# A hybrid decoder block on one core: a new order of the opening, an earlier projection chunk, and the first queries' scores in two products

## The chip, the cores and the metric

The kernel runs on one core of one Trainium2 chip. The metric is the device time of one execution in microseconds (us); the time of a kernel is the median of its runs. The core has a matrix engine (TensorE, in the profile PE, its weight loads PEld), a vector engine (VectorE, DVE), a scalar engine for copies and functions (ScalarE, ACT), a general engine (GpSimd, POOL) and SyncE (SP), which here only issues DMAs. Each works through its own queue in order and waits on semaphores for the others.

## What is computed

One decoder layer over 512 tokens of width 1024, all in float32:

```
h = rms_norm(x, norm_mix_g)
q_a,k_a,v_a,o_a,i_a,f_a,q_b,k_b,v_b,g_a,g_b = split(h @ w_in)      # 8208 columns
q_a,k_a = silu(causal_conv(concat(q_a,k_a), conv_w))
y_a = sigmoid(o_a) * head_rms_norm(mlstm_chunkwise(q_a,k_a,v_a,i,f))     # 8 heads, 64 wide keys, 128 wide values
y_b = stick_breaking(head_rms_norm(q_b), head_rms_norm(k_b), v_b)        # 8 heads, 128 wide
y = sigmoid(g_a + b) * y_a + sigmoid(g_b + b) * y_b
x = x + y @ w_out
x = x + square(relu(rms_norm(x, norm_mlp_g) @ w_up)) @ w_down
```

The stick-breaking attention takes, for a query t, beta = sigmoid(q.k / sqrt(128)) for all keys before t, and weights v_s with beta_ts times the product of (1 - beta_tj) over the keys j between s and t.

## The kernel before

**Products in three parts.** Every float32 operand is split into an upper part (`hi`, a copy by ACT into a type that TensorE takes) and a lower part (`lo`, value minus `hi`, by DVE). `mm3` (line 119) then issues three matrix products into one accumulator: hi x hi, hi x lo, lo x hi. Nearly all products are 128 x 128 stationary by 512 moving columns.

**Chunks.** A projection of 512 columns is a chunk (`chunk`, line 124): four accumulators of 128 x 512 in the pool `ps_proj` (4 PSUM banks), eight steps k over the 1024 inputs, so 8 x 4 x 3 = 96 products. Weights come in four loads of 256 rows (`stage`, line 103): SP issues the DMA into a `raw` buffer, ACT makes `hi` and DVE makes `lo`. `raw` has two buffers (three from chunk `qkb1` on, line 663), `hi` and `lo` four each.

**The order of the work.** The list `ORDER` (line 60) names steps, and `step` (line 660) issues each: `qka` are the mLSTM's q and k projections with their convolution, `r` its decay tables, `m` its heads, `n` its norm; `qkb`, `T` and `s` are the attention's q and k projections, the transposes of a pair of heads and a head; `va`, `vb`, `oa`, `ga`, `gb` the other projections. The order of the list is a priority: a scheduler places instructions on the engines' queues at compile time, higher priority first, but lets a later step's instructions go ahead where they are ready and an earlier step's aren't. `tc.high_priority` moves instructions up, `tc.issue_after(i)` puts them behind `i` on its engine. A tile whose pool has no free buffer waits for one.

**The opening** (lines 185 to 384) computes `h` transposed (`hT`, upper and lower) and at the same time the first chunk, `va0`. SP loads, for four tiles of 128 tokens, `x` (512 KB each) and, for each 256 rows of `va0`'s weights, `raw_va` (512 KB each), in turns. The string given to `opening` (line 370) is the order on ACT and DVE, written by hand: `q` t squares and sums tile t on ACT and takes root and reciprocal (line 256); `s` t g scales half g of tile t on DVE into `xn`, and PE turns it with four transposes of 128 x 128 (line 263); `u` t g and `l` t g write the upper and lower part of that half of `hT` (ACT, DVE); `w` i and `v` i the upper and lower part of weight pair i; `g` the gate weights. `in_turn` (line 248) puts each step behind the last one on its engine.

PE meanwhile runs filler products on a tile of zeros into the bank `pw` (`keep_warm`, line 229): eight at the start, two after the gain rows, then 1, 5 and 3 after the transposes of (0, 0), (0, 1) and (1, 0) (line 274). `va0`'s accumulators: two of `ps_proj`'s four banks are `gps`, the gain rows, which are read until tile 3 is scaled; accumulators 0 and 1 have the two others. `behind` (line 372) puts the steps k = 4 to 7 of `va0` behind the transposes of tiles 2 and 3.

**An attention head** (`sb_head`, line 548) takes scores of four blocks of 128 queries against their 512, 384, 256 and 128 keys. `SEG` names the segments: j = 0 has 512 columns at offset 0, j = 1 has 384 at 512, j = 3 has 128 at 896, j = 2 has 256 at 1024. Three banks hold them (`half_square`, line 85), so the first 128 queries (j = 3) lie behind j = 1 in the second bank, and half of the third bank is empty. ACT reads each segment twice for sigmoid(z) and sigmoid(-z), POOL masks the diagonal, DVE scans, PE transposes (`zt`) and multiplies with v (`po`).

Of the kernel before, what the change touches and what calls it, by code (L numbers as in the profile page):

```python
# [8 lines left out]
F32 = mybir.dt.float32  # L9
F32R = mybir.dt.float32r  # L10
# [46 lines left out]
C_QB, C_KB, C_VB, C_GA, C_GB = 3088, 4112, 5136, 6160, 7184  # L57


ORDER = ("qka0 r0 r1 qkb0 m0 r2 m1 r3 T0 qkb1 m2 m3 n0 vb0 s0 T1 s1 oa0 s2 s3 qka1 ga0 r4 r5 va1 m4 r6 m5 r7 qkb2 m6 m7 "  # L60
         "n4 T2 qkb3 vb1 s4 s5 T3 gb0 s6 s7 x0 oa1 ga1 gb1").split()


# [1 line left out]
def block_kernel(ctx: ExitStack, tc: tile.TileContext, x, norm_mix_g, w_in, b_if, b_gate, conv_w, mlstm_norm_g,  # L65
# [32 lines left out]
        return at.tile([P, S], F32, tag=tag, name=name, bufs=bufs)  # L98


    last, load_pool, staged = {}, [(wp, "raw", 2)], []

    def stage(k2, srcs, name, ahead=None, pool_raw=None):

        with tc.high_priority(offset=AHEAD if ahead is None else ahead):
            p, tag, bufs = load_pool[len(staged) % len(load_pool)] if pool_raw is None else (pool_raw, "raw", 2)
            staged.append(name)
            raw = p.tile([P, 2, 512], F32, tag=tag, name=f"raw_{name}{k2}", bufs=bufs)
            for c, ap in srcs:
                n = ap.shape[-1]  # L110
                last["load"] = nc.sync.dma_start(out=raw[:, :, c:c + n],
                                                 in_=ap.rearrange("(kk p) n -> p kk n", p=P)).ins
            hi = wp.tile([P, 2, 512], F32R, tag="whi", name=f"whi_{name}{k2}")
            lo = wp.tile([P, 2, 512], F32R, tag="wlo", name=f"wlo_{name}{k2}")
            act.copy(hi, raw)  # L115
            dve.tensor_sub(lo, raw, hi.bitcast(F32))  # L116
        return hi, lo

    def mm3(o, ah, al, bh, bl, start, stop, **kw):
        pe.matmul(o, ah, bh, start=start, stop=False, **kw)  # L120
        pe.matmul(o, ah, bl, start=False, stop=False, **kw)  # L121
        return pe.matmul(o, al, bh, start=False, stop=stop, **kw).ins  # L122

    def chunk(name, src, transposed, lhs=None, staged=None, evac=None, gen=False,
              order=range(4), behind={}):


        acc = {}

        def one(o, k, wh, wl):  # L130
            kk, sl = k % 2, slice(o * P, (o + 1) * P)
            st, sp = k == 0, k == NK - 1
            if transposed:
                mm3(acc[o], wh[:, kk, sl], wl[:, kk, sl], hT[0][:, k, :], hT[1][:, k, :], st, sp)
            else:
                ah, al = (hT[0][:, k, sl], hT[1][:, k, sl]) if lhs is None else lhs(k, sl)
                mm3(acc[o], ah, al, wh[:, kk, :], wl[:, kk, :], st, sp)

        def new(o):
            acc[o] = ps_proj.tile([P, S], F32, tag="pp", name=f"pp_{name}{o}")  # L140

        if evac is not None:
            w = staged or [stage(k2, src(k2), name) for k2 in range(4)]
            def each():
                for o in order:
                    new(o)
                    for k in range(NK):
                        with ExitStack() as es:
                            if k in behind:
                                es.enter_context(tc.issue_after(behind[k]))  # L150
                            one(o, k, *w[k // 2])
                    evac(o, acc[o])
                    yield
            if gen:
                return each()
            list(each())
        else:
            for o in range(4):
# [32 lines left out]
    gx = xp.tile([1, D], F32, name="gx")  # L191
    nc.sync.dma_start(out=gx, in_=norm_mix_g[0:1, :])
    xs, raw_va, va0_src = {}, {}, in_cols((C_VA, 512))
    for i in range(NT):
        xs[i] = xp.tile([P, D], F32, name=f"x_{i}")
        nc.sync.dma_start(out=xs[i], in_=x[0, i * P:(i + 1) * P, :])
        raw_va[i] = (xp if i < 2 else wp).tile([P, 2, 512], F32, tag="raw", name=f"raw_va0{i}", bufs=2)
        last["load"] = nc.sync.dma_start(out=raw_va[i], in_=va0_src(i)[0][1].rearrange("(kk p) n -> p kk n", p=P)).ins
    eps = cst.tile([P, 1], F32, name="eps")
    pool.memset(eps, EPS)  # L200
    one1 = xp.tile([P, P], F32R, name="one1")
# [27 lines left out]
    def keep_warm(n):  # L229
        for i in range(n):  # L230
            pe.matmul(pw, warm[:, :P], warm, start=True, stop=True)
# [31 lines left out]
    def o_scale(t, g):  # L263
        if g == 0:
            xn_[t] = xp.tile([P, D], F32, tag="nx", name=f"xn{t}", bufs=3)
        c = slice(g * S, (g + 1) * S)
        yield dve.scalar_tensor_tensor(xn_[t][:, c], xs[t][:, c], r_[t], gps[g], ALU.mult, ALU.mult).ins
        pt_[t, g] = bank(f"pt{t}{g}")
        for i in range(4):
            k = 4 * g + i  # L270
            turned = pe.transpose(pt_[t, g][:, i * P:(i + 1) * P], xn_[t][:, k * P:(k + 1) * P], ident).ins
        last["turned", t, g] = turned
        with tc.issue_after(turned):
            keep_warm({(0, 0): 1, (0, 1): 5, (1, 0): 3}.get((t, g), 0))

    def h_part(t, g):
        return [h[:, 4 * g:4 * g + 4, t * P:(t + 1) * P] for h in hT], pt_[t, g][:, :].rearrange(
# [7 lines left out]
        (hi, lo), p3 = h_part(t, g)  # L285
        yield dve.tensor_sub(lo, p3, hi.bitcast(F32)).ins

    def o_weights(i):
        va0_w[i] = tuple(wp.tile([P, 2, 512], F32R, tag=f"w{w}", name=f"w{w}_va0{i}") for w in ("hi", "lo"))
        yield act.copy(va0_w[i][0], raw_va[i]).ins  # L290

    def o_weights_lower(i):
        yield dve.tensor_sub(va0_w[i][1], raw_va[i], va0_w[i][0].bitcast(F32)).ins  # L293
# [72 lines left out]
    with tc.issue_after(last["load"]):  # L366
        nc.sync.dma_start(out=wr, in_=w_in[0, :, C_I:C_I + 16].rearrange("(k p) n -> p k n", p=P))
    wg = r4.tile([P, 2, S], F32R, tag="r4", name="wg")[:, :, :].rearrange("p w (k n) -> p (w k) n", k=4)
    pool.memset(wg.bitcast(F32), 0.0)
    opening("q0 s00 s01 u00 l00 w0 v0 q1 s10 u01 l01 s11 u10 l10 w1 v1 u11 l11 q2 s20 s21 w2 v2 u20 l20 q3 s30 u21 "  # L370
            "s31 l21 w3 v3 u30 g l30 u31 l31")
    va0 = chunk("va0", None, False, staged=va0_w, evac=v_evac(v0, "va0"), gen=True,
                behind={k: last["turned", k // 2, 1] for k in range(4, NK)})
    next(va0)
    next(va0)
    next(va0)
# [171 lines left out]
    def sb_head(h, q, k, rq, v):  # L548

        z = half_square(f"zb{h}_")  # L550
        for j, o, n in SEG:
            il = slice((3 - j) * P, (4 - j) * P)
            mm3(part(z, o, n), q[:, 0, il], q[:, 1, il], k[:, 0, :n], k[:, 1, :n], j != 3, True,
                skip_group_check=True)
        b, r = f5(f"b{h}"), f5(f"r{h}")
        for j, o, n in SEG:
            for w, d in ((1, r), (0, b)):
                act.activation(d[:, o:o + n], part(z, o, n), AF.Sigmoid, scale=rq[:, w, 3 - j, h % 2:h % 2 + 1])  # L558
        for j, o, n in SEG:
            d = slice(o + n - P, o + n)  # L560
            pool.affine_select(out=b[:, d], in_=b[:, d], pattern=[[-1, P]], compare_op=ALU.is_gt, fill=0.0, base=0,  # L561
# [87 lines left out]
        pool.memset(oh[:, h, h:h + 1], 1.0)  # L649
    oh_r = at.tile([P, 8, 8], F32R, name="oh_r")  # L650
    pool.tensor_copy(oh_r, oh)
    msk = at.tile([P, S], F32, name="msk")
    pool.memset(msk, 0.0)
    pool.memset(msk[:, 384:], 1.0)
# [336 lines left out]
```

## Time and profile before

| | us |
|---|---|
| median of 3 runs | 816.85 (816.73 to 817.37) |
| the profiled execution | 816.42 |
| span of its instructions | 814.4 |

The profile is of one execution. Its span runs from the first to the last instruction; what is left of the execution's time lies around it. A row of a timeline has the start, the time until the end, engine, line of the kernel, operation, what it writes and reads, the count of instructions merged into the row, and in brackets how long the engine was idle before it and what ended that. Ends of matrix products are modelled and overlap the next one's start, so the distance from start to start tells their cost. In a row of waits stand the engine and line that waited, what it waited for, us in total, times, and the longest. A row of a window has the stretch and its length, then for each engine its busy time and count, PE's clock, the DMA share and GB/s. What a load took from issue to landing is the last number of its row in the DMA view.

### The profile page before, as it was taken

How to read it: one execution, taken by the hardware profiler on the slowest of the kernel's cores; microseconds unless marked ns; L12 is line 12 of the kernel's file. 1: busy time of each engine (PE TensorE's matmuls, PEld its weight loads, DVE VectorE, ACT ScalarE, POOL GpSimd, SP SyncE). 2: the span in 40 equal slices, each digit the busy share in tenths (PEclk: the TensorE clock that was granted, in tenths of full speed). 3: DMA queues.
4: the chain of work that ended last, by engine and by line, in shares of the span. 5: the costliest groups of instructions: out<-in, count | busy, mean ns of one | idle time of the engine just before them, and what ended most of it. 6: DMA issues, size and time to landing. Idle time of an engine off the chain costs nothing.

```text
span 814.4 us, 11569 instructions
## 1 busy us (share of the span) xinstructions
PE 805.7 (99%) x4392; PEld 693.5 (85%) x4392; DVE 599.8 (74%) x828; ACT 457.1 (56%) x681; POOL 164.6 (20%) x216
## 2 busy tenths in 40 slices
PE   8999999999999999999999999999999999999998
PEld 6878887888888887888888888999999899999876
DVE  6669967684598486756753659898689868978995
ACT  6429756654557467545542537576455635755642
POOL 3014323111221240010120101223302330232220
PEclk9999999999999999999999999999999999999999
DMA  9454542343433423522257506987977995999964
GB/s 225 98 155 147 123 77 63 88 98 85 150 93 93 120 62 70 137 72 77 78 182 263 124 1 158 208 177 159 204 228 161 179 208 182 182 198 184 233 120 119
DMA packets 64552, 113.65 MB, mean 140 GB/s; under 512 B 5809, under 2 KB 18401, under 8 KB 64498
## 3 DMA queue, kind: packets, MB, share of 16 engines
q1 hardware_dynamic: 44914, 71.43, 31.6%
q0 software_dynamic: 19584, 41.50, 26.8%
q8 instruction: 34, 0.56, 0.3%
q14 instruction: 20, 0.16, 0.1%
HBM read 110.74 MB, written 2.17 MB: 139 GB/s over the span
## 4 chain that ended last, share of the span: by engine, by line
PE 92%; DVE 5%; ACT 1%; issue 1%; DMA 0%; SPq 0%; DVEq 0%; ACTq 0%
PE pp_qkb L122 4%; PE pp_qkb L120 4%; PE pp_qkb L121 4%; PE pp_yup L120 3%; PE pp_yup L121 3%; PE pp_yup L122 3%; PE ydn L121 2%; PE ydn L122 2%; PE ydn L120 2%; PE pp_qka L120 2%; PE pp_va L121 2%; PE pp_qka L121 2%; PE pp_ga L121 2%; PE pp_vb L122 2%; PE pp_vb L120 2%; PE pp_oa L122 2%
## 5 line engine op out<-in xcount | busy, mean ns | idle before, releaser
L561 POOL TENSOR_SCALAR_AFFINE_SELECT b<-b 128x128 f32<-128x128 f32 x32 | 19.0, 608 | 161.2 <-ACT b L558 161.2
L121 PE MATMUL pp_qkb<-wlo_qkb,hT 128*128 128x512 f32 x128 | 50.2, 392 | 0.0
L122 PE MATMUL pp_qkb<-whi_qkb,hT 128*128 128x512 f32 x128 | 50.1, 394 | 0.0
L120 PE MATMUL pp_qkb<-whi_qkb,hT 128*128 128x512 f32 x128 | 49.4, 392 | 0.0
L767 POOL DMA_DIRECT2D raw_Xup<-in_w_up_dram x24 | 28.9, 1239 | 84.8 <-DVE wlo_p5up L728 37.2
L767 POOL DMA_DIRECT2D raw_Xdn<-in_w_down_dram x18 | 21.6, 1214 | 102.8 <-DVE wlo_p5dn L728 36.4
L566 DVE TENSOR_TENSOR_SCAN r<-r,msk 128x512 f32<-128x512 f32 (+3 forms) x32 | 25.1, 833 | 14.5 <-ACT r L558 14.5
L116 DVE TENSOR_TENSOR wlo_qkb<-raw_qkb,whi_qkb 128x1024 fp32r<-128x1024 f32 x16 | 21.7, 1364 | 13.8 <-ACT whi_qkb L115 13.8
L122 PEld LDWEIGHTS pp_qkb<-whi_qkb,hT 128*128 128x128 f32 x128 | 24.1, 188 | 5.1
L120 PEld LDWEIGHTS pp_qkb<-whi_qkb,hT 128*128 128x128 f32 x128 | 24.1, 188 | 5.1
L121 PEld LDWEIGHTS pp_qkb<-wlo_qkb,hT 128*128 128x128 f32 x128 | 24.1, 188 | 4.7
L913 ACT ACTIVATE uq<-uq 128x512 f32<-128x512 f32 x32 | 20.0, 630 | 12.2 <-DVE uq L912 12.0
L121 PE MATMUL pp_va<-wlo_va,hT 128*128 128x512 f32 x64 | 24.9, 392 | 0.8 <-DVE wlo_va L293 0.8
L120 PE MATMUL pp_ga<-hT,whi_ga 128*128 128x512 f32 x64 | 25.3, 395 | 0.0
L120 PE MATMUL pp_qka<-hT,whi_qka 128*128 128x512 f32 x64 | 25.2, 397 | 0.0
L121 PE MATMUL pp_qka<-hT,whi_qka 128*128 128x512 f32 x64 | 25.2, 394 | 0.0
L121 PE MATMUL pp_wo<-wlo_wo,y 128*128 128x512 f32 x64 | 25.1, 392 | 0.0
L121 PE MATMUL pp_ga<-hT,whi_ga 128*128 128x512 f32 x64 | 25.1, 392 | 0.0
L121 PE MATMUL pp_oa<-hT,whi_oa 128*128 128x512 f32 x64 | 25.1, 392 | 0.0
L122 PE MATMUL pp_oa<-hT,wlo_oa 128*128 128x512 f32 x64 | 25.1, 392 | 0.0
L120 PE MATMUL pp_vb<-whi_vb,hT 128*128 128x512 f32 x64 | 25.1, 392 | 0.0
L121 PE MATMUL pp_gb<-hT,whi_gb 128*128 128x512 f32 x64 | 25.1, 392 | 0.0
(578 smaller groups left out, 2962.1 us busy)
## 6 DMA issues: line engine op xcount, KB each, us to landing
raw_Xup<-in_w_up_dram POOLq DMA_DIRECT2D x24, 512.0 KB, 7.3
raw_Xdn<-in_w_down_dram POOLq DMA_DIRECT2D x18, 512.0 KB, 6.6
raw_qkb<-in_w_in_dram SPq DMA_DIRECT2D x32, 256.0 KB, 3.9
rb<-rows POOLq DMA_DIRECT2D x8, 640.0 KB, 5.5
raw_va<-in_w_in_dram SPq DMA_DIRECT2D x8, 512.0 KB, 5.2
raw_qka<-in_w_in_dram SPq DMA_DIRECT2D x16, 256.0 KB, 6.3
raw_vb<-in_w_in_dram SPq DMA_DIRECT2D x8, 512.0 KB, 4.4
raw_oa<-in_w_in_dram SPq DMA_DIRECT2D x8, 512.0 KB, 4.2
```

The lines of the kernel that those rows point to most:

```text
L116: dve.tensor_sub(lo, raw, hi.bitcast(F32))
L120: pe.matmul(o, ah, bh, start=start, stop=False, **kw)
L121: pe.matmul(o, ah, bl, start=False, stop=False, **kw)
L122: return pe.matmul(o, al, bh, start=False, stop=stop, **kw).ins
L561: pool.affine_select(out=b[:, d], in_=b[:, d], pattern=[[-1, P]], compare_op=ALU.is_gt, fill=0.0, base=0, channel_multiplier=1)
L566: dve.tensor_tensor_scan(kr, kr, msk[:, S - n:][:, ::-1], 1.0, ALU.mult, ALU.max)
L767: pool.dma_start(out=buf[b, j], in_=src(more, j), accum_op=ALU.add)
L913: act.activation(h(r, c), h(r, c), AF.Square)
```

## The change

Four edits.

1. **Opening.** Loads go x0 x1 w0 w1 x2 w2 x3 w3 instead of x0 w0 x1 w1 and so on. The hand-written order takes x1's square and the transposes of tile 1 ahead of the first weights, and splits weight pairs 0 to 2 into halves (`w00` is the first 128 rows of pair 0). Fillers after (0, 1) are three, not five. In `va0` lo x hi stands before hi x lo (`rows_first`, with the roles as in `mm3`'s arguments). Accumulator 2 takes the fillers' bank `pw`, and tile 1's step k = 3 is put behind the transposes of tile 2's first half.
2. **ORDER.** `qka1` moves from behind `s3` to ahead of `s1`.
3. **A third raw buffer** for the third load of `qkb0`, in the pool `at` (`at_once`).
4. **First queries' scores.** In `sb_head` segment j = 3 goes into the empty half of the third bank: q hi against both parts of the keys in one product of 256 columns, then q lo against k hi, 128 columns. ACT copies the first 128 columns to `b`, DVE adds the second 128, and the two sigmoids read `b`.

```diff
-ORDER = ("qka0 r0 r1 qkb0 m0 r2 m1 r3 T0 qkb1 m2 m3 n0 vb0 s0 T1 s1 oa0 s2 s3 qka1 ga0 r4 r5 va1 m4 r6 m5 r7 qkb2 m6 m7 "
+ORDER = ("qka0 r0 r1 qkb0 m0 r2 m1 r3 T0 qkb1 m2 m3 n0 vb0 s0 T1 qka1 s1 oa0 s2 s3 ga0 r4 r5 va1 m4 r6 m5 r7 qkb2 m6 m7 "
...
+            p, tag, bufs = at_once.get((name, k2), (p, tag, bufs))
...
+    at_once["qkb0", 2] = (at, "raw", 1)
...
-    def mm3(o, ah, al, bh, bl, start, stop, **kw):
+    def mm3(o, ah, al, bh, bl, start, stop, rows_first=False, **kw):
         pe.matmul(o, ah, bh, start=start, stop=False, **kw)
-        pe.matmul(o, ah, bl, start=False, stop=False, **kw)
-        return pe.matmul(o, al, bh, start=False, stop=stop, **kw).ins
+        two = ((ah, bl), (al, bh))
+        for i, (a, b) in enumerate(two[::-1] if rows_first else two):
+            end = pe.matmul(o, a, b, start=False, stop=stop and i == 1, **kw).ins
+        return end
...
-                mm3(acc[o], ah, al, wh[:, kk, :], wl[:, kk, :], st, sp)
+                mm3(acc[o], ah, al, wh[:, kk, :], wl[:, kk, :], st, sp, name == "va0")
...
-            acc[o] = ps_proj.tile([P, S], F32, tag="pp", name=f"pp_{name}{o}")
+            acc[o] = banks.get(o) or ps_proj.tile([P, S], F32, tag="pp", name=f"pp_{name}{o}")
...
-                            if k in behind:
-                                es.enter_context(tc.issue_after(behind[k]))
+                            for i in (k, (o, k)):
+                                if i in behind:
+                                    es.enter_context(tc.issue_after(behind[i]))
...
-    for i in range(NT):
+    for n in "x0 x1 w0 w1 x2 w2 x3 w3".split():
...
-            keep_warm({(0, 0): 1, (0, 1): 5, (1, 0): 3}.get((t, g), 0))
+            keep_warm({(0, 0): 1, (0, 1): 3, (1, 0): 3}.get((t, g), 0))
...
-    def o_weights(i):
-        va0_w[i] = tuple(wp.tile([P, 2, 512], F32R, tag=f"w{w}", name=f"w{w}_va0{i}") for w in ("hi", "lo"))
-        yield act.copy(va0_w[i][0], raw_va[i]).ins
+    def o_weights(i, h=None):
+        if not h:
+            va0_w[i] = tuple(wp.tile([P, 2, 512], F32R, tag=f"w{w}", name=f"w{w}_va0{i}") for w in ("hi", "lo"))
+        c = slice(None) if h is None else slice(h, h + 1)
+        yield act.copy(va0_w[i][0][:, c], raw_va[i][:, c]).ins
...
-    opening("q0 s00 s01 u00 l00 w0 v0 q1 s10 u01 l01 s11 u10 l10 w1 v1 u11 l11 q2 s20 s21 w2 v2 u20 l20 q3 s30 u21 "
-            "s31 l21 w3 v3 u30 g l30 u31 l31")
-    va0 = chunk("va0", None, False, staged=va0_w, evac=v_evac(v0, "va0"), gen=True,
-                behind={k: last["turned", k // 2, 1] for k in range(4, NK)})
+    opening("q0 s00 s01 q1 u00 s10 l00 s11 w00 u10 v00 w01 l10 v01 u01 u11 l01 l11 w10 v10 w11 v11 q2 s20 s21 w20 u20 v20 "
+            "w21 l20 v21 q3 s30 s31 u21 l21 w3 v3 u30 g l30 u31 l31")
+
+    va0 = chunk("va0", None, False, staged=va0_w, evac=v_evac(v0, "va0"), gen=True, banks={2: pw}, behind={
+        **{k: last["turned", k // 2, 1] for k in range(4, NK)}, (1, 3): last["turned", 2, 0]})
...
-        for j, o, n in SEG:
+        for j, o, n in sorted(SEG)[:3]:
             il = slice((3 - j) * P, (4 - j) * P)
-            mm3(part(z, o, n), q[:, 0, il], q[:, 1, il], k[:, 0, :n], k[:, 1, :n], j != 3, True,
-                skip_group_check=True)
+            mm3(part(z, o, n), q[:, 0, il], q[:, 1, il], k[:, 0, :n], k[:, 1, :n], True, True, skip_group_check=True)
+
+        x = z[2][0][:, HT:].rearrange("p (w n) -> p w n", w=2)
+        pe.matmul(x, q[:, 0, :P], k[:, :, :P], start=False, stop=False, skip_group_check=True)
+        pe.matmul(x[:, 0, :], q[:, 1, :P], k[:, 0, :P], start=False, stop=True, skip_group_check=True)
         b, r = f5(f"b{h}"), f5(f"r{h}")
+        act.copy(b[:, OFF[3]:OFF[3] + P], x[:, 0, :])
+        dve.tensor_add(b[:, OFF[3]:OFF[3] + P], x[:, 1, :], b[:, OFF[3]:OFF[3] + P])
         for j, o, n in SEG:
             for w, d in ((1, r), (0, b)):
-                act.activation(d[:, o:o + n], part(z, o, n), AF.Sigmoid, scale=rq[:, w, 3 - j, h % 2:h % 2 + 1])
+                act.activation(d[:, o:o + n], part(z, o, n) if j != 3 else b[:, o:o + n], AF.Sigmoid,
+                               scale=rq[:, w, 3 - j, h % 2:h % 2 + 1])
```

More of the change, by code (lines that the diff above doesn't have):

```diff
@@ L98, in t2 @@
         return at.tile([P, S], F32, tag=tag, name=name, bufs=bufs)
-    last, load_pool, staged = {}, [(wp, "raw", 2)], []
+    last, load_pool, staged, at_once = {}, [(wp, "raw", 2)], [], {}
     def stage(k2, srcs, name, ahead=None, pool_raw=None):
@@ L117, in stage @@
         return hi, lo
-    def mm3(o, ah, al, bh, bl, start, stop, **kw):
+    def mm3(o, ah, al, bh, bl, start, stop, rows_first=False, **kw):
         pe.matmul(o, ah, bh, start=start, stop=False, **kw)
-        pe.matmul(o, ah, bl, start=False, stop=False, **kw)
-        return pe.matmul(o, al, bh, start=False, stop=stop, **kw).ins
+        two = ((ah, bl), (al, bh))
+        for i, (a, b) in enumerate(two[::-1] if rows_first else two):
+            end = pe.matmul(o, a, b, start=False, stop=stop and i == 1, **kw).ins
+        return end
     def chunk(name, src, transposed, lhs=None, staged=None, evac=None, gen=False,
-              order=range(4), behind={}):
+              order=range(4), behind={}, banks={}):
         acc = {}
@@ L193, in block_kernel @@
     xs, raw_va, va0_src = {}, {}, in_cols((C_VA, 512))
-    for i in range(NT):
[L195 to L198, printed above, removed]
+    for n in "x0 x1 w0 w1 x2 w2 x3 w3".split():
+        i = int(n[1])
+        if n[0] == "x":
+            xs[i] = xp.tile([P, D], F32, name=f"x_{i}")
+            nc.sync.dma_start(out=xs[i], in_=x[0, i * P:(i + 1) * P, :])
+        else:
+            raw_va[i] = (xp if i < 2 else wp).tile([P, 2, 512], F32, tag="raw", name=f"raw_va0{i}", bufs=2)
+            last["load"] = nc.sync.dma_start(out=raw_va[i],
+                                             in_=va0_src(i)[0][1].rearrange("(kk p) n -> p kk n", p=P)).ins
     eps = cst.tile([P, 1], F32, name="eps")
@@ L286, in o_lower, with o_weights_lower @@
         yield dve.tensor_sub(lo, p3, hi.bitcast(F32)).ins
-    def o_weights(i):
-        va0_w[i] = tuple(wp.tile([P, 2, 512], F32R, tag=f"w{w}", name=f"w{w}_va0{i}") for w in ("hi", "lo"))
-        yield act.copy(va0_w[i][0], raw_va[i]).ins
-    def o_weights_lower(i):
-        yield dve.tensor_sub(va0_w[i][1], raw_va[i], va0_w[i][0].bitcast(F32)).ins
+    def o_weights(i, h=None):
[3 more added lines that the diff above has]
+        yield act.copy(va0_w[i][0][:, c], raw_va[i][:, c]).ins
+    def o_weights_lower(i, h=None):
+        c = slice(None) if h is None else slice(h, h + 1)
+        yield dve.tensor_sub(va0_w[i][1][:, c], raw_va[i][:, c], va0_w[i][0][:, c].bitcast(F32)).ins
     def o_gates():
```

## The prediction

> **What bounds the kernel now.** The profiled execution took 816.42 us, of which the span of its instructions is 814.4; the median of the three timed runs is 816.85. The sum below is a difference, taken within the 816.42, and is then put on the median. I began with the page: busy time first, then the chain that ended last.
>
> ```profile
> span 814.4 us, 11569 instructions
> PE 805.7 (99%) x4392; PEld 693.5 (85%) x4392; DVE 599.8 (74%) x828; ACT 457.1 (56%) x681; POOL 164.6 (20%) x216
> PE 92%; DVE 5%; ACT 1%; issue 1%; DMA 0%; SPq 0%; DVEq 0%; ACTq 0%
> ```
>
> TensorE (PE) is busy for 805.7 of 814.4 us and is 92% of the chain. So only two things can save time: fewer or shorter PE instructions, or less PE idle time. The view of PE's own waits says where the idle time is:
>
> ```profile
> PE pw L231 <- DVE warm L190: 1.5, 1, 1.5
> PE pt L271 <- DVE xn L267: 0.9, 1, 0.9
> PE pp_va L121 <- DVE wlo_va L293: 0.8, 1, 0.8
> ```
>
> The view has eight rows, and the five left out are 0.4 us or less each, all in the MLP part from 487 us on. No row belongs to a projection chunk of the middle or to an attention head: from 12 to about 487 us PE never waits. The only idle time that this diff touches is 0.9 + 0.8 us in the opening. To it come the filler products on `warm` (L231), which are busy time without use.
>
> **The opening.** I read PE in order of time for the first 20 us (start, us, what):
>
> ```profile
> 1.54 3.44 PE L231 MATMUL pw<-warm 128*128 128x512 f32 x8 [1.54 <-DVE warm L190]
> ...
> 7.25 0.66 PE L271 MATMUL pt<-ident,xn 128*128 128x128 f32 x4 [0.88 <-DVE xn L267]
> ...
> 8.33 1.41 PE L231 MATMUL pw<-warm 128*128 128x512 f32 x5
> ...
> 10.79 0.50 PE L121 MATMUL pp_va<-wlo_va,hT 128*128 128x512 f32 x1 [0.77 <-DVE wlo_va L293]
> ...
> 12.46 0.94 PE L231 MATMUL pw<-warm 128*128 128x512 f32 x3
> ...
> 18.02 1.03 PE L271 MATMUL pt<-ident,xn 128*128 128x128 f32 x8
> 18.81 0.71 PE L120 MATMUL pp_va<-whi_va,hT 128*128 128x512 f32 x2
> ```
>
> After 13.4 us PE has no hole. At 18.81 the first products with the third pair of weight rows (w2) begin; by then PE has done all 24 transposes of token tiles 0 to 2 and the 24 products of tiles 0 and 1 with weights w0 and w1. That set of work is my mark: whatever the new order does, the opening gains as much as the mark comes earlier, provided that no hole follows. What the mark depends on are the loads and the ScalarE (ACT) and VectorE (DVE) queues. Issues on SP, then landings from four narrow windows of the DMA view (x0, w0, x1, x2, each found at its issue time; the last number is us from issue to landing):
>
> ```profile
> 1.23 0.36 SPq L196 DMA_DIRECT2D x<-in_x_dram  x1
> 1.64 0.42 SPq L198 DMA_DIRECT2D raw_va<-in_w_in_dram  x1
> 2.10 0.47 SPq L196 DMA_DIRECT2D x<-in_x_dram  x1
> ...
> 3.09 1.59 SPq L196 DMA_DIRECT2D x<-in_x_dram  x1
> ...
> x<-in_x_dram SPq DMA_DIRECT2D x1, 512.0 KB, 3.3
> raw_va<-in_w_in_dram SPq DMA_DIRECT2D x1, 512.0 KB, 6.6
> x<-in_x_dram SPq DMA_DIRECT2D x1, 512.0 KB, 7.4
> x<-in_x_dram SPq DMA_DIRECT2D x1, 512.0 KB, 10.9
> ```
>
> So x0 lands at 4.5, w0 at 8.2, x1 at 9.5, x2 at 14.0. The diff exchanges w0 and x1, and only these two. An x behind a w took 1.3 us more (9.5 less 8.2), so I estimate x1 at 4.5 + 1.3 = 5.8 and w0 at 9.5, the place that x1 had. What lies behind them is the same bytes: x2 stays at 14.0.
>
> ```profile
> 7.94 0.58 ACT L282 CAST hT<-pt 128x512 fp32r<-128x512 f32 x1 [1.79 <-PE pt L271]
> ...
> 14.65 1.07 ACT L259 ACTIVATE jk<-x 128x1024 f32<-128x1024 f32 x1
> ...
> 15.85 0.29 ACT L260 ACTIVATE r<-r,eps 128x1 f32<-128x1 f32 x1
> ...
> 16.17 0.16 DVE L261 RECIPROCAL r<-r 128x1 f32<-128x1 f32 x1
> 16.37 1.41 DVE L267 SCALAR_TENSOR_TENSOR xn<-x,r,gps 128x512 f32<-128x512 f32 x2
> ```
>
> Here x2 landed at 14.0 but its square began at 14.65: ACT, which works in order, was still on tile 1. In the new order tile 1's square, its two copies of `hT` and four half copies of weights stand ahead of q2. Followed by these rows: x1's square and root take 15.85 + 0.29 - 14.65 = 1.5 us. They start when ACT is free after tile 0's root (7.94 - 1.79 = 6.15) and are through by 7.7, inside the hole of 1.79 us before the first copy of `hT`, which needs the transposes of 7.25. A half copy of weights I take as the 0.58 us of that copy of 512 columns. The half copy w00 waits for w0 (9.5) and with it u10, w01, u01, u11 behind it on ACT and v00, l10, v01 on DVE, and the first products start near 10.2 instead of 9.6. But then both tiles are there: from the landing of w0 PE has 12 products in one go (12 x 0.23 = 2.8 us, 10.2 to about 13.4 with four transposes). w1 I take at 12.7, one x (1.3) ahead of x2, as before; its first half is cast by 13.4, and 9 of its 12 products run until about 15.6. The last three (tile 1, k = 3) now wait by order behind tile 2's first transposes.
>
> x2's square can now start at 14.05, since ACT has finished w11 by about 13.95. The same steps as above follow 0.6 us earlier: root at 15.25, first half of `xn` at 15.8 to 16.5, transposes at 16.6 and, for the second half, 17.3. PE has nothing to do from 15.6 to 16.6, fills the space between the two transposes with the three products held back, and reaches the mark at 16.6 + 0.4 + 0.7 + 0.4 = about 18.2, instead of 18.81. **Term 1: -0.6 us.** Two of the filler products fewer is inside it. Behind the mark there is no hole: at 18.2 there are six products per weight half and, since accumulator 2 now has the bank of `pw` and needn't wait for `gps`, 12 more of tile 2. Bounds: if x2's row were later by 0.6 the gain is nothing; at best it is all of the holes and fillers that are left, 0.9 + 0.8 + 1.4 + 0.9 (the five and three fillers) = 4.0. The value nearest to the rows is 0.6.
>
> **A rule on the clock.** The 19 filler products exist to keep PE active, and the change takes two away and opens a 1.0 us hole. In the trace the first eight fillers take 3.44 / 8 = 0.43 us each and later products 0.23, and that pace holds through the holes of 0.88 and 0.77 us. (The profile's row of granted clock doesn't tell the two apart; the durations do.)
>
> ```profile
> PEclk9999999999999999999999999999999999999999
> ```
>
> So I charge the new hole with its own length alone. A fall back to 0.43 for one stretch as long as the first (3.44 us) would cost half of it, 1.7 us: rival (d). The Trainium skill, TensorE: Matmul & The Clock Gate, Part 1, has this as a rule: idle for a window of about 3.4 us that runs on its own count, PE goes back to half clock. By that rule a hole of 1.0 us alone doesn't trip it, which gives the sum as it stands, and a window that counted as idle would give (d).
>
> **First queries' scores.** Attention heads score the first 128 queries in three products of 128 columns:
>
> ```profile
> 147.89 0.22 PE L120 MATMUL zb<-kT,qT 128*128 128x128 f32 x1
> 147.95 0.27 PE L121 MATMUL zb<-kT,qT 128*128 128x128 f32 x1
> 148.06 0.27 PE L122 MATMUL zb<-kT,qT 128*128 128x128 f32 x1
> 148.17 0.33 PE L120 MATMUL zb<-kT,qT 128*128 128x256 f32 x1
> ...
> 165.75 0.28 PE L121 MATMUL po<-al,vb 128*128 128x256 f32 x1
> 165.87 0.28 PE L122 MATMUL po<-ah,vb 128*128 128x256 f32 x1
> ...
> 166.16 0.28 PE L122 MATMUL po<-ah,vb 128*128 128x128 f32 x1
> 166.27 0.30 PE L537 MATMUL pt_qT<-ident,nat 128*128 128x128 f32 x1
> ```
>
> From start to start they take 148.17 - 147.89 = 0.28 us. In their place come one product of 256 columns (0.12, from 165.75 to 165.87) and one of 128 with other stationary operand (0.11, 166.16 to 166.27, or 0.06, as from 147.89 to 147.95). Saved: 0.05 to 0.10 a head, times eight. **Term 2: -0.4 us**, the lower end, because the last product is followed by a change of weights as in the 166.16 row; at most -0.8. The copy and the addition of 128 columns that put the two halves together are new on ACT and DVE, about 0.4 and 0.3 us a head by the nearest rows of their size (mean ns after the bar):
>
> ```profile
> L558 ACT ACTIVATE b<-zb,rq 128x128 f32<-128x128 f32 x8 | 3.1, 390 | 0.0
> L531 DVE TENSOR_SCALAR nat<-nat,ssq 128x128 f32<-128x128 f32 x32 | 8.3, 330 | 0.0
> ```
>
> They lie beside the chunk that PE works on meanwhile (in s1's stretch, quoted at rival (c), PE is busy 19.10 of 19.10 us). Without that cover they would cost 0.7 x 8 = 5.6 us.
>
> **qka1 ahead of s1, the third buffer.** Nothing is added or removed: 96 products, eight loads of 256 KB on SP, taps, sigmoids and splits move forward past s1, oa0, s2 and s3. SP has qka1's loads behind oa0's, and the new order takes them first; POOL has four clears of `ql`, past the masks of the heads. As PE has no hole there, the gain is nothing, and I take 0. The buffer for the third `qkb0` load releases a load that no product waited for: 0.
>
> **Sum:** -0.6 - 0.4 = -1.0; 816.42 becomes 815.4 in a profile, and the median 816.85 becomes **815.8 us**. What can be told from no change is 0.2%, 1.6 us, so the likeliest verdict is the same.
>
> **Rivals.** (a) The opening gains more, 1.2 to 2.5 us: x2 lands earlier, since x0 and x1 now stream back to back, or the two-tile start fills holes that I left. For it: PE would have 21 of the 24 products done by 15.6, three us ahead of the mark. Against it: x2 has the same bytes ahead of it. Middle 1.8, with term 2: 814.6.
>
> (b) The opening doesn't do what its order says, and gains nothing: x1 doesn't come early (queue order or contention), and ACT, where u00 and w00 stand behind x1's square, is held. It decides from x1 after about 8.5, and at its old 9.5 the mark comes some 1 us later than before, 19.9: 816.85 + 1.1 - 0.4 = 817.5; midway, 816.6.
>
> (c) Slower: the moved conv takes DVE ahead of s1's chain, and PE waits at `zt`. Busy time by stretch (PE, PEld, DVE, ACT, POOL), during qka0's conv and in s1's stretch, and of qka1's conv alone where it is now (DVE, ACT):
>
> ```profile
> 60.00:80.00 20.00, 20.00 (x90) 16.57 (x89) 17.85 (x28) 17.90 (x31) 10.03 (x18) 1.00 0.52 170
> ...
> 172.30:191.40 19.10, 19.10 (x97) 15.98 (x95) 12.53 (x16) 10.45 (x19) 2.12 (x4) 1.00 0.40 73
> ...
> 177.80:256.30 78.50, 19.62 (x32) 7.36 (x12) 1.00 0.32 93
> ```
>
> 19.6 us of conv meet 19.10 - 12.53 = 6.6 free ones: s1 comes up to 13 us later. A whole next chunk (96 x 0.23 = 22 us) covers that; if only half of one is at hand (11), PE waits 2 us, and as s2's chain is pushed as well, twice: 816.85 - 1.0 + 4 = 819.9. It decides once s1's lag is over the products at hand. Against it: in qka0's conv DVE was at 17.85 of 20, and PE didn't wait.
>
> (d) PE falls back to the pace of its first eight products for 3.44 us in the opening, +1.7: 816.85 - 1.0 + 1.7 = 817.5. Against it: it kept its pace through both old holes.
>
> **Chances.** Forecast 0.48 (its own range 815.2 to 816.5), (a) 0.30, (b) 0.12, (c) 0.06, (d) 0.04. Faster by over 0.2% (below 815.2) is (a), 0.30; slower (above 818.5) is (c), 0.06; the rest, 0.64, is the same. The range takes in the forecast, (b) and (d) up to 817.5 and (a) down to 814.0; (c) and the tail of (a) are left out.
>
> **What would show it.** Right: the square of x2 at 14.0 to 14.1, a PE hole of about 1 us before tile 2's transposes, first products with w2 at about 18.2, and 0.23 us a head for the first queries. Term 1 is wrong if x1 lands after 8 or x2 before 13; term 2 if the pair takes 0.28; the zero for qka1 if a PE wait on `zt`, `po` or a chunk turns up between 150 and 480 us.

## The result, and the profile after

| | before | after |
|---|---|---|
| median, us | 816.79 (816.45 to 817.37, 4 runs) | 822.55 (821.21 to 822.8, 4 runs) |
| the profiled execution, us | 816.42 | 821.21 |
| span of its instructions, us | 814.4 | 819.3 |
| mean granted PE clock | 0.999 | 0.997 |

The changed kernel is slower by 0.66%: ratio 1.0066, 95% interval 1.0049 to 1.0084. The forecast was 815.8 with a range of 814.0 to 817.5. The page of the changed kernel, with the lines that answer to those of before:

```profile
span 819.3 us, 11574 instructions
PE 806.8 (98%) x4382; PEld 694.0 (85%) x4382; DVE 599.6 (73%) x839; ACT 457.5 (56%) x690; POOL 161.3 (20%) x216
PE 88%; DVE 5%; DMA 4%; ACT 1%; issue 1%; SPq 0%; ACTq 0%; DVEq 0%
```

The page's chain has something new: DMA has 4% of it, where it had 0%. PE is busy 1.1 us longer with ten instructions fewer, so some of them ran slower. The view of PE's waits, its three longest:

```profile
PE pp_qkb L121 <- ACT xc L405: 4.0, 1, 4.0
PE pw L239 <- DVE warm L194: 1.5, 1, 1.5
PE pt L279 <- DVE xn L275: 1.3, 2, 1.0
```

The first row is where the loss begins. Before, no projection chunk of the middle waited; now `qkb0` waits 4.0 us for ACT to copy the accumulators of `qka0` (`xc`). PE's timeline there, and then three windows of 3.41 us around it (stretch, length, busy time and count of PE, PEld, DVE, ACT and POOL, granted clock, DMA share, GB/s):

```profile
62.51 0.39 PE L124 MATMUL pp_qka<-hT,wlo_qka 128*128 128x512 f32 x1
66.92 0.50 PE L121 MATMUL pp_qkb<-whi_qkb,hT 128*128 128x512 f32 x1 [4.02 <-ACT xc L405]
...
69.91 0.63 PE L124 MATMUL pp_qkb<-whi_qkb,hT 128*128 128x512 f32 x1
70.33 0.63 PE L121 MATMUL pp_qkb<-whi_qkb,hT 128*128 128x512 f32 x1
...
71.14 0.40 PE L124 MATMUL pp_qkb<-whi_qkb,hT 128*128 128x512 f32 x1
71.38 0.40 PE L121 MATMUL pp_qkb<-whi_qkb,hT 128*128 128x512 f32 x1
```

```profile
60.85:64.26 3.41, 2.05 (x10) 1.35 (x8) 0.00 (x0) 0.00 (x0) 2.48 (x10) 1.00 0.97 370
64.26:67.67 3.41, 0.76 (x3) 0.66 (x4) 1.26 (x2) 2.34 (x4) 2.56 (x7) 1.00 0.16 56
67.67:71.08 3.41, 3.41 (x9) 2.65 (x9) 3.37 (x7) 3.41 (x8) 0.77 (x2) 0.50 0.40 79
```

After the hole the granted clock is 0.50 for 3.41 us, and products come every 0.42 us (69.91 to 70.33) instead of every 0.24 (71.14 to 71.38). For PE that is half of 3.41, 1.7 us, on top of the 4.0. Now ACT, which works in order, first before and then after:

```profile
57.72 1.05 ACT L115 CAST whi_qkb<-raw_qkb 128x1024 fp32r<-128x1024 f32 x1 [5.94 <-PE pp_qka L121]
61.34 1.95 ACT L393 COPY xc<-pp_qka 128x512 f32<-128x512 f32 x3 [2.58 <-PE pp_qka L122]
63.19 1.05 ACT L115 CAST whi_qkb<-raw_qkb 128x1024 fp32r<-128x1024 f32 x1
64.13 0.60 ACT L393 COPY xc<-pp_qka 128x512 f32<-128x512 f32 x1
64.61 5.55 ACT L443 ACTIVATE rb<-rb,cc 128x512 f32<-128x512 f32 x12
...
71.47 0.63 ACT L405 ACTIVATE xc<-cy 128x512 f32<-128x512 f32 x1
```

```profile
65.33 1.04 ACT L116 CAST whi_qkb<-raw_qkb 128x1024 fp32r<-128x1024 f32 x1 [14.00 <-DMA raw_qkb<-in_w_in_dram]
66.28 1.56 ACT L405 COPY xc<-pp_qka 128x512 f32<-128x512 f32 x3
67.72 1.07 ACT L116 CAST whi_qkb<-raw_qkb 128x1024 fp32r<-128x1024 f32 x1
68.67 0.60 ACT L405 COPY xc<-pp_qka 128x512 f32<-128x512 f32 x1
69.14 5.56 ACT L455 ACTIVATE rb<-rb,cc 128x512 f32<-128x512 f32 x12
...
76.01 0.63 ACT L417 ACTIVATE xc<-cy 128x512 f32<-128x512 f32 x1
```

The queue is the same: cast of `qkb0`'s third weights, three copies of accumulators, cast of the fourth, the last copy, twelve exponentials of the decay rows, the first sigmoid of the convolution. But the third cast stands idle for 14.0 us for its load, and all the others stand behind it. The load is the one that edit 3 moved. Its buffer in `at` lies on memory that the opening's gate tiles held, so SP waits for PE to be done with them before it can issue the load (SP's waits between 50 and 60 us):

```profile
SPq L112 <- DVE wlo_qkb L117: 8.6, 1, 8.6
SPq L112 <- PE pc L356: 1.0, 1, 1.0
SPq L112 <- DMA rows<-cm: 0.2, 1, 0.2
```

Before, its two halves were issued at 52.01 and 52.41 and landed at 55.9 and 56.5, ahead of all broadcasts. After, the fourth load goes first and the third is issued at 53.37 and 53.78, beside POOL's three broadcasts of decay rows (52.89, 53.49, 54.02; 640 KB each), and is there at 65.3.

The parts that were forecast in numbers are x2's square in ACT's timeline, and in PE's tile 2's first transposes, the mark, and the first queries' scores.

```profile
14.33 1.06 ACT L267 ACTIVATE jk<-x 128x1024 f32<-128x1024 f32 x1 [0.33 <-DMA x<-in_x_dram]
```

```profile
16.93 0.63 PE L279 MATMUL pt<-ident,xn 128*128 128x128 f32 x4 [1.01 <-DVE xn L275]
...
18.44 0.48 PE L121 MATMUL pp_va<-whi_va,hT 128*128 128x512 f32 x1
...
153.77 0.28 PE L568 MATMUL zb<-kT,qT 128*128 128x256 f32 x1
153.89 0.22 PE L569 MATMUL zb<-kT,qT 128*128 128x128 f32 x1
153.94 0.40 PE L506 MATMUL pq<-sh,oh_r 128*8 128x512 f32 x1
```

The mark, PE's first product with the third pair of weight rows, came at 18.44 instead of 18.81, a gain of 0.37. The pair of score products takes 153.94 - 153.77 = 0.17 us instead of 0.28.

### The profile page after: what moved, and what is told of

Read it like the earlier page. It is cut to its first block, busy times and chain, and to the rows that moved or that the text cites. A ratio compares the mean times of both kernels' runs of the same rounds, so it can differ in the third digit from the quotient of the medians.

```text
span 819.3 us, 11574 instructions
## 1 busy us (share of the span) xinstructions
PE 806.8 (98%) x4382; PEld 694.0 (85%) x4382; DVE 599.6 (73%) x839; ACT 457.5 (56%) x690; POOL 161.3 (20%) x216
## 4 chain that ended last, share of the span: by engine, by line
PE 88%; DVE 5%; DMA 4%; ACT 1%; issue 1%; SPq 0%; ACTq 0%; DVEq 0%
PE pp_qkb L124 7%; PE pp_yup L124 5%; PE ydn L124 4%; PE pp_qkb L121 4%; PE pp_vb L124 4%; PE pp_gb L124 4%; PE pp_ga L124 4%; PE pp_oa L124 4%; PE pp_xup L124 4%; PE pp_zup L124 3%; PE zdn L124 3%; PE pp_wo L124 3%; PE pp_va L124 3%; PE pp_yup L121 3%; PE xdn L124 3%; PE ydn L121 2%
## 5 line engine op out<-in xcount | busy, mean ns | idle before, releaser
L116 ACT CAST whi_qkb<-raw_qkb 128x1024 fp32r<-128x1024 f32 x16 | 16.9, 1054 | 21.5 <-DMA raw_qkb<-in_w_in_dram 14.0
L124 PE MATMUL pp_qka<-hT,whi_qka 128*128 128x512 f32 x64 | 25.4, 396 | 0.0
L121 PE MATMUL pp_oa<-hT,whi_oa 128*128 128x512 f32 x64 | 25.2, 394 | 0.0
L124 PE MATMUL pp_oa<-hT,whi_oa 128*128 128x512 f32 x64 | 25.2, 394 | 0.0
L124 PE MATMUL pp_ga<-hT,wlo_ga 128*128 128x512 f32 x64 | 25.1, 393 | 0.0
L124 PE MATMUL pp_gb<-hT,wlo_gb 128*128 128x512 f32 x64 | 25.0, 391 | 0.0
L124 PE MATMUL pp_vb<-wlo_vb,hT 128*128 128x512 f32 x64 | 25.0, 391 | 0.0
```

The costliest lines, as they stand in the source:

```text
L124: end = pe.matmul(o, a, b, start=False, stop=stop and i == 1, **kw).ins
```

## The experiments

Each kernel of the table is described below it, and compared with the kernel before on the same chip in the same set of runs; line numbers in rows shift with each edit. Two numbers go with most of the times: when ACT's first sigmoid of `qka0`'s convolution starts, and when PE starts the last four transposes of the keys of the first attention pair (`pt_kT`), about 34 us later. Both are from the timelines of the profiled executions. They don't order all kernels: l_cast_silu has an early sigmoid and a loss, and b_at_once_only, whose `pt_kT` is 1.6 us behind that of the changed kernel, ends no later.

| kernel | first sigmoid | last `pt_kT` | apart | median us, less that of before | ratio, interval |
|---|---|---|---|---|---|
| before | 71.47 | 105.92 | 34.45 | | |
| after | 76.01 | 111.44 | 35.43 | +5.76 | 1.0066, 1.0049 to 1.0084 |
| a_no_at_once | 74.91 | 109.16 | 34.25 | +1.64 | 1.0018, 1.0010 to 1.0027 |
| b_at_once_only | 79.04 | 113.07 | 34.03 | +5.54 | 1.0064, 1.0052 to 1.0076 |
| d_rb_behind | 74.28 | 108.64 | 34.36 | +1.62 | 1.0016, 1.0007 to 1.0025 |
| e_fill | 76.25 | 111.77 | 35.52 | +5.23 | 1.0066, 1.0052 to 1.0080 |
| f_opening_only | 74.05 | 108.34 | 34.29 | +2.07 | 1.0025, 1.0016 to 1.0034 |
| g_load_order | 71.20 | 105.56 | 34.36 | -0.95 | 0.9989, 0.9980 to 0.9998 |
| h_swap_only | 75.23 | 109.42 | 34.19 | +3.17 | 1.0038, 1.0024 to 1.0051 |
| i_move_scores | 71.93 | 106.21 | 34.28 | -0.72 | 0.9991, 0.9983 to 1.0000 |
| m_opening_order | 71.31 | 105.77 | 34.46 | -0.05 | 0.9995, 0.9987 to 1.0004 |
| c_own_buffer | 73.77 | 108.14 | 34.37 | +1.10 | 1.0011, 1.0002 to 1.0019 |
| k_cast_behind | 73.81 | 108.53 | 34.72 | +2.26 | 1.0024, 1.0014 to 1.0033 |
| l_cast_silu | 70.49 | 111.56 | 41.07 | +2.88 | 1.0036, 1.0024 to 1.0048 |
| n_own_behind | 70.80 | 105.25 | 34.45 | -1.87 | 0.9976, 0.9966 to 0.9986 |

### Is it the third buffer?

**b_at_once_only** is the kernel before with edit 3 alone, **a_no_at_once** the changed kernel without it.

```diff
-    at_once["qkb0", 2] = (at, "raw", 1)
```

> The kernel before with the third edit alone. Theory (placement): the hole of about 4 us before qkb0's first product appears here too, with a stretch at half clock, and the median is 821.5 to 823.5. Rival (another edit): no hole, 816.5 to 817.1.

> The change without its third edit: the third load of qkb0 goes to the pool of two raw buffers again. Theory (placement): the loss is all in this edit, since its buffer lies on memory that the opening still reads, so the load comes late, meets the rb loads, holds ACT and through it PE, and PE falls to half clock. Then the hole of 4.0 us and the 3.4 us at half clock are gone, no PE wait over 0.5 us stands between 12 and 480 us, and the median is 815.2 to 816.4. Rival (another edit: the opening's order or qka1 ahead of s1): the hole stays and the median is 820 or more.

Edit 3 alone makes the whole loss: 822.51, with a PE wait of 3.7 us for `xc` and a half clock for 3.41 us from 68.42 on. That it is at fault is shown. But a_no_at_once, where the hole near 63 us is gone, missed its range: without edit 3 the changed kernel is still 1.64 us slower than before, at 818.61, where a gain of 1 had been forecast. So there was a second loss, which the first one covered.

**d_rb_behind** keeps the third load on `at`'s memory, late as it is, and holds the three broadcasts back until it has landed.

```diff
+            if h < 3:
+                es.enter_context(tc.issue_after(pool.tensor_copy(loaded["seen"], loaded["raw"][:, 1, 511:]).ins))
             nc.gpsimd.dma_start(out=rb, in_=rows[h:h + 1, :].partition_broadcast(P))
```

> The changed kernel; the third qkb0 load has the same late buffer, but the first three rb loads on GpSimd wait until it has landed (GpSimd copies a column of it first). Theory (the late load is slow because it shares the DMA engines with 1.9 MB of rb loads): it is issued at 53 to 54 us as before, lands within 5 us instead of 12, the PE hole falls below 0.5 us, and the median is 815.2 to 817. Rival (the late issue alone is enough): a hole of 2 us or more stays, and the median is 819 or more.

The third load was there for a cast at 58.43 and PE's hole was gone, so the load was late because of the broadcasts, and not because of its issue 1.4 us later alone. The time, 818.59, missed: the broadcasts were now late themselves, the exponentials waited five times, 2.4 us in all, for the masks that POOL lays on them, and the first sigmoid came at 74.28.

**e_fill** fills the hole with 17 products.

```diff
+        if i == 0:
+            fill = bank("fill")
+            for _ in range(17):
+                pe.matmul(fill, hT[0][:, 0, :P], hT[0][:, 0, :], start=True, stop=True)
```

> The changed kernel with 17 products into a spare bank, results unused, between qka0 and qkb0 on PE, so that PE has work in the hole; ACT and the load are left as they are. Theory (part of the loss is PE at half clock after the hole): the first product of qkb0 comes as late as in the changed kernel (66.9), but the clock stays at 1.0, and the median falls by 1.5 to 3.5 us, to 819.0 to 821.0. Rival (the slow pace after the hole is not the clock's): the median stays at 822 or more.

The clock stayed at 1.0 in the profile, as expected, and the time missed the range: 822.2, no better than the changed kernel. In this run, then, PE's half clock was not what bounded the end. With PE at full speed `qkb0` ends earlier, but the keys of the first pair are turned at 111.77, as late as without the filling (111.44), after new waits of 0.9 us (`pt_kT`) and 0.8 us (`pn`, the mLSTM's norm). The sigmoid at 76.25 bounds them: 34.3 us behind it, the distance of the runs without a hole, is 110.6, so at most 0.9 us was to be had. So two delays lay side by side in the changed kernel, PE's own 5.7 us and ACT's and DVE's 4.5, and taking 1.7 from the first uncovers the second. Why this run doesn't reach even 110.6 was not taken apart; the filling changed the orders of ACT (its first three sigmoids stand in a row), DVE and PE as well. So it doesn't show that the clock is free. The executions of one kernel speak against that: of b_at_once_only's five, the one with a mean clock of 1.0 took 821.14 and the two with 0.995 took 822.99 and 823.62; the changed kernel took 821.21 at 0.997 and 822.36 to 822.8 at 0.995. What the half clock costs in the end time stays open.

### Where is the second loss?

It lies between 62.8 and 109 us: in a_no_at_once and d_rb_behind DVE waits there for the first sigmoid (2.67 us in d_rb_behind), and everything behind it on DVE is late by as much. What holds ACT in a_no_at_once is the cast of the *fourth* weights of `qkb0`, which waits 2.94 us for its load. In SP's queue as built, the first half of the load of `qkb1`'s third weights, which also goes to `at` and waits for PE's gate transposes (`pc`), had come to stand ahead of that fourth load. Before, it stood behind it. The scheduler's order had flipped; kernels built with one edit each show that the opening does it, 40 us ahead of the place. Four runs test it, with the move and the scores as the rival.

**f_opening_only** is the kernel before with edit 1. **h_swap_only** is the kernel before with nothing but the swap in SP's queue:

```diff
+            if (name, k2) == ("qkb0", 3):
+                early["raw"] = at.tile([P, 2, 512], F32, tag="raw", name="raw_qkb12", bufs=1)
+                early["load"] = nc.sync.dma_start(out=early["raw"][:, :, :256], ...).ins
...
+                with tc.issue_after(early["load"]) if (name, k2) == ("qkb0", 3) else ExitStack():
```

**g_load_order** is a_no_at_once with the old order held by one edge:

```diff
+                with tc.issue_after(last["qkb03"]) if (name, k2) == ("qkb1", 2) else ExitStack():
```

**i_move_scores** is the kernel before with edits 2 and 4, and **m_opening_order**, run later, the kernel before with edit 1 and that edge.

> The kernel before with the new opening alone. Theory Q: the new opening reorders SP's queue as well. The first half of the load of qkb1's third weights, which waits for PE's four gate transposes, now stands ahead of the two halves of qkb0's fourth load, so that this one is issued behind the first broadcast of decay rows and lands near 66.5 us instead of 61.7; ScalarE's cast of it and what stands behind the cast (a copy, twelve exponentials, the first silu) run about 3 us late, and 2.5 of that reaches PE at the transposes of the first attention pair near 105 us. It expects 818.4 to 819.4 us, with a wait of 2 to 4 us of ScalarE for raw_qkb near 64 us. Rival R: the loss that is left without the third buffer comes from the moved chunk or the new scores; then the opening alone gives its own gain and ends at 816.0 to 816.7.

> The kernel before with that swap of SP's queue and nothing else: the first half of the load of qkb1's third weights ahead of qkb0's fourth load; the orders of the four other engines stay those of before. Theory Q expects 818.8 to 819.8 (the kernel before plus 2 to 2.8 us). Rival R expects 816.5 to 817.3, no change.

> The changed kernel without the third buffer, with one edge more: the load of qkb1's third weights stands behind the load of qkb0's fourth in SP's queue, as it did before the change; PE's, ScalarE's, VectorE's and POOL's orders stay those of the changed kernel without the third buffer. Theory Q expects the fourth load near 61 to 62 us, no wait of ScalarE for it above 1 us, and the sum that was forecast: 815.4 to 816.4. Rival R expects 818.2 to 819.0, as without the edge.

> The kernel before with the moved chunk and the new scores, with the old opening and no third buffer; SP's queue keeps its order up to qkb1. Theory Q expects the gain of the scores alone, 816.2 to 817.0, with no new wait. Rival R expects the loss here: 818.3 to 819.5.

> The kernel before with the new opening and the edge that keeps SP's queue in its old order; neither the moved chunk nor the new scores nor the third buffer. Theory Q expects the opening's own gain alone, 0.2 to 0.8 us: 816.2 to 816.9. Rival R, by which the new opening costs something besides SP's order, expects 817.3 or more.

All but the sizes of h_swap_only (820.21, just above its range) and m_opening_order (817.02) came out as the theory of the queue had them, and against the rival. The row that tells it is the cast of the fourth weights in ACT's timeline, in h_swap_only and then in g_load_order:

```profile
66.93 1.06 ACT L121 CAST whi_qkb<-raw_qkb 128x1024 fp32r<-128x1024 f32 x1 [3.51 <-DMA raw_qkb<-in_w_in_dram]
```

```profile
62.91 1.06 ACT L118 CAST whi_qkb<-raw_qkb 128x1024 fp32r<-128x1024 f32 x1
```

One swap of two loads, with the orders of PE, ACT, DVE and POOL left as they were, costs 3.17 us; the edge takes the loss of a_no_at_once back and lets the forecast sum of -1.0 appear, -0.95. The move and the scores together give -0.72 (interval 0 to -1.4), with no new wait; the opening with the old queue can't be told from no change (-0.05 by the medians, +0.3 to -1.1 by the interval).

### Place of the buffer, place in the queue

**k_cast_behind** and **l_cast_silu** leave the changed kernel's load as late as it is and move ACT's cast of it: behind the four copies of accumulators, or behind the first sigmoid.

```diff
+            if (name, k2) == ("qkb0", 2):
+                with tc.issue_after(last["xc"]):
+                    act.copy(hi, raw)
+                with tc.issue_after(last["cy"]):
+                    dve.tensor_sub(lo, raw, hi.bitcast(F32))
```

> The changed kernel, its late load left as late as it is, with ScalarE's cast of it and the cast of the fourth moved behind the four copies of the accumulators of qka0. Theory P says that PE's hole comes only from the cast standing ahead of those copies in ScalarE's queue: PE's wait near 63 us is then under 0.5 us and the clock stays at 1.0. The casts still hold the twelve exponentials and the first silu back until 65 us and two casts more, so that the silu starts about 3 us later than in the kernel before, and PE loses 2 to 3 us at the first attention pair: 817.6 to 819.0. A rival T (the half clock, and not the late silu, is what the hole cost) expects 815.3 to 816.8, because with the hole gone the clock is full.

> As the last one, but with the two casts behind the exponentials and the first silu as well; the load is as late as in the changed kernel. Theory P expects the first silu near 71.3 us as in the kernel before (71.47), the second about a cast and a half later, at most 1 us of PE waits for the late weights of qkb0, and 815.6 to 817.4. If the load's lateness itself, and not its place in the queue, makes the loss, 818 or more.

k_cast_behind has no wait of PE near 63 us and yet is slow, because ACT's exponentials stand behind the late cast (its row in ACT's timeline) and the sigmoid comes at 73.81:

```profile
65.05 1.05 ACT L118 CAST whi_qkb<-raw_qkb 128x1024 fp32r<-128x1024 f32 x1 [1.49 <-DMA raw_qkb<-in_w_in_dram]
```

So the hole is the work of the cast's place. The median of 819.33 lies above the range. Six of the twelve runs have a mean clock of 0.997 or 0.998 and take 819.37 us or more, the six others 0.999 or 1.0 and take 817.51 to 819.3. The rival that only the clock counted expected 816.8 at most with a full clock; these six lie above that, so the late sigmoid is enough for a loss, but the size of the median is in part the clock's. Where the first six lose the clock no trace shows; the profile, which is of one of the others, has a wait of 1.22 us at 104.03 (`pt_qT`).

l_cast_silu missed, 819.95: the load's lateness costs even with its cast out of the way. The sigmoid came early, at 70.49, but the late cast frees its `raw` buffer late, SP waits 8.4 us for DVE's `wlo` of it, and the next loads are late in turn. In ACT's timeline a cast waits for one of them, and in PE's follow two holes:

```profile
82.57 1.06 ACT L122 CAST whi_qkb<-raw_qkb 128x1024 fp32r<-128x1024 f32 x1 [5.75 <-DMA raw_qkb<-in_w_in_dram]
```

```profile
85.65 0.50 PE L471 MATMUL za<-qh,kk 128*128 128x512 f32 x1 [0.79 <-DVE kk L440]
...
88.96 0.79 PE L127 MATMUL pp_qkb<-whi_qkb,hT 128*128 128x512 f32 x1 [1.76 <-ACT nat L536]
```

**c_own_buffer** gives the third load memory that nothing else uses, so that it waits for no reader, and one edge puts it right behind the second load in SP's queue, ahead of the fourth.

```diff
+                with tc.issue_after(last["load"]) if (name, k2) == ("qkb0", 2) else ExitStack():
...
+    own = under.enter_context(tc.tile_pool(name="own", bufs=1, side="right", reuse_waits="tile"))
...
-    at_once["qkb0", 2] = (at, "raw", 1)
+    at_once["qkb0", 2] = (own, "raw", 1)
```

> The changed kernel with the third buffer on memory that nothing else uses, so that qkb0's third load waits for no transpose and no scores, and is issued ahead of the fourth. Theory P (the loss of the third buffer comes from the memory that it was given, over the gate tiles of the opening) expects both loads landed before 58 us, no wait of PE above 0.5 us near 63 us, the clock at 1.0 throughout, and 815.2 to 816.5. Rival S (a third load in flight there costs by itself, by contention with the decay rows or by the shifted queue) expects 818 or more.

Its third load landed at 46.29, there was no hole and no half clock, with the orders of PE, ACT, DVE and POOL those of the changed kernel: the memory, with the place in SP's queue that it costs, was the fault, as expected. But 818.17 missed, and is where rival S had it, by contention with the decay rows. Now the *broadcasts* were late, landing at 62.50, 64.50 and 66.42 (59.79, 62.02 and 63.99 in g_load_order), since with one buffer more the loads of `qkb1`'s first and third weights were issued from 52.05 on, just ahead of them and among them. In ACT's timeline the exponentials wait for the masks that POOL lays on the broadcast rows:

```profile
63.78 1.92 ACT L457 ACTIVATE rb<-rb,cc 128x512 f32<-128x512 f32 x4
67.09 1.79 ACT L457 ACTIVATE rb<-rb,cc 128x512 f32<-128x512 f32 x3 [1.39 <-POOL rb L451]
```

**n_own_behind** is that kernel with these two loads on POOL's queue, behind the third broadcast.

```diff
+                behind = (name, k2) in (("qkb1", 0), ("qkb1", 2))
...
+                      tc.issue_after(last["rb2"]) if behind else ExitStack()):
+                    l = (nc.gpsimd if behind else nc.sync).dma_start(out=raw[:, :, c:c + n], ...).ins
```

> The changed kernel with the third buffer on memory of its own, and the loads of qkb1's first and third weights issued on POOL's queue behind the third broadcast of decay rows instead of on SP's queue beside the first; the orders of PE, ScalarE and VectorE are those of the run with the buffer of its own. Theory U (the first silu, 34.3 us ahead of the last transposes of the first attention pair in every run so far, sets the time, and in the run with the buffer of its own it was late because loads of qkb1 were issued ahead of the broadcasts) expects the broadcasts to land by 64.2 us, the silu by 71.3 us and 815.2 to 816.6. Rival V (the third buffer costs in another way) expects 817.5 to 818.7, the time without this edit.

The broadcasts landed at 59.05, 60.59 and 62.18, the two loads behind them by 65.13, the exponentials ran without a wait, and the sigmoid came at 70.80 (ACT's timeline):

```profile
63.94 5.56 ACT L461 ACTIVATE rb<-rb,cc 128x512 f32<-128x512 f32 x12
69.51 1.28 ACT L423 ACT_TABLE_LOAD   x1
70.80 0.63 ACT L423 ACTIVATE xc<-cy 128x512 f32<-128x512 f32 x1
```

At 815.32 us this is the fastest kernel here, 0.24% below the one before (0.14% to 0.34%).

The Trainium skill, DMA: Bandwidth & Descriptors, section "Queues, rings and completion order", says that each DMA engine takes turns between the queues for which it has work. The landings agree: broadcasts on POOL's queue lost time to loads on SP's queue issued among them (the third landed at 66.42), and landed earliest with the same loads put behind them on their own (62.18).

## Why the prediction was wrong

**The step that failed** is its last zero: "The buffer for the third `qkb0` load releases a load that no product waited for: 0." It priced what the edit might release and not what it takes: the memory that the new buffer lies on, and who still reads it; the place in SP's queue that the load loses while it waits; the broadcasts that get ahead of it; and what stands behind its cast on ACT. The memory and its readers can be read in the kernel, and what stands behind the cast in ACT's timeline of before; the place in the queue shows once the kernel is built. In place of 0 the edit cost 5.5 us (b_at_once_only).

**A second step failed unseen.** Term 1 counted what the opening's edit issues inside the opening, and no queue behind it. The scheduler orders the whole program, and the edit at 10 us swapped two loads at 54 us. Worth 3.17 us alone (h_swap_only), it accounts for the loss that is left without the third buffer.

**What let both pass** was the reading that PE never waits from 12 to 487 us. That is true, and it says nothing of slack. Before, the first sigmoid and the last `pt_kT` are 34.45 us apart, and in the six kernels with a late sigmoid and no PE hole near 63 us (a, c, d, f, h and k) they are 34.2 to 34.7. So before the change ACT's and DVE's chain met PE with next to nothing to spare, some 0.2 us as estimated from most of the six (34.2 to 34.4).

**Term 1**, -0.6: the mechanism was right, with the hole of 1.01 us and tile 2's transposes as foretold; only the landing of x2 was off. In the eleven profiles with the new opening x2's square starts between 13.94 and 15.16, and the mark follows 4.11 to 4.13 us behind it, at 18.05 to 19.29. Against the 18.81 of before the term was -0.37 in the changed kernel's profile, and anything from -0.76 to +0.48 in the others.

**Term 2**, -0.4: too small. The pair takes 0.17 us and not 0.23, since the last product costs 0.05, as the row of 147.89 had it, and not 0.11: 8 x 0.11 = -0.9. That is not all: the first product of 256 columns behind the three took 0.17 us (148.17 to 148.34) and takes 0.12 now, so a whole head's scores, from their first product to the next operation, fall from 1.97 to 1.82 us, which makes -1.2 over eight. The copy and the addition made no wait in i_move_scores.

**The zero for qka1** held in i_move_scores, which has no wait on `zt`, `po` or a chunk. But the sign that the prediction named against it did turn up: in the changed kernel PE waits 0.26 us on `po` at 171.0. Of the nine other kernels with edits 2 and 4 seven have it too, 0.3 to 0.6 us in most and 1.42 in n_own_behind, where PE is 2.9 us earlier at `pt_kT` than in c_own_buffer (0.4); no kernel without these edits has it. Whether the moved chunk or the new scores make it was not taken apart.

**The rivals.** (a) and (c) didn't occur. (b), an opening that gains nothing, m_opening_order's interval can't exclude, though the mark was earlier in ten of the eleven profiles. (d), the half clock, did, but in `qkb0`. Its price of 1.7 us was right for PE alone; what it is worth in the end time, with the sigmoid late as well, these runs leave open.

## What to carry to other kernels

A buffer more is a place in memory and a place in a queue: ask which earlier tiles lie there, what the load is now issued behind, and what stands behind the instruction that waits for it on an engine that works in order. "PE never waits" doesn't say how far the engines behind it are from making it wait; measure the distance between a marker on the feeding engine and one on PE, which was 34.2 to 34.7 us in eleven of the fifteen kernels here. And after any edit, compare the built order of all queues with that of before, far from the edit too: here a swap of two loads 40 us behind it cost three times what all four edits were to gain.

## What was not expected of the hardware

The clock fell without an idle stretch as long as its window. In l_cast_silu PE waited 0.79 us, ran eight products and waited 1.76 us; its windows are

```profile
81.77:85.18 3.41, 3.09 (x14) 2.24 (x12) 1.49 (x2) 2.56 (x4) 0.00 (x0) 1.00 0.40 112
85.18:88.59 3.41, 1.55 (x8) 1.26 (x8) 3.29 (x5) 3.31 (x6) 0.00 (x0) 1.00 0.75 129
88.59:92.00 3.41, 3.04 (x7) 2.46 (x8) 3.32 (x6) 3.39 (x7) 0.10 (x1) 0.50 0.66 119
```

A window in which PE was busy for 1.55 of 3.41 us (45%) was followed by one at half clock; in the changed kernel it was 0.76 of 3.41 (22%), while a window with 2.05 us (60%) ahead of it was not. In b_at_once_only the two cases lie side by side:

```profile
61.60:65.01 3.41, 1.67 (x8) 1.05 (x6) 0.00 (x0) 0.00 (x0) 1.24 (x5) 1.00 0.90 347
65.01:68.42 3.41, 1.45 (x6) 1.24 (x7) 1.96 (x3) 3.03 (x5) 3.09 (x8) 1.00 0.03 10
68.42:71.83 3.41, 3.41 (x9) 2.67 (x8) 3.41 (x6) 3.41 (x8) 0.19 (x1) 0.50 0.54 122
```

A window with 1.67 us (49%) kept the full clock behind it, the next one with 1.45 (43%) lost it. So in these profiles the line lies between 45% and 49% of a window; the ends of products are modelled, so the shares are rough. The rule that the prediction cites (the Trainium skill, TensorE: Matmul & The Clock Gate, Part 1) has the window and its own count, and the lengths agree; that a window nearly half busy counts as idle is what these runs add. It would explain how a hole of 3.7 us, or a shorter one, can cost the clock in one execution and not in another, as the mean clocks of b_at_once_only's five (0.995 to 1.0) differ; that was not tried.
